# Transposes of a pair's two heads issued as one group of eight

## The chip, the cores and the metric

The kernel runs on one core of a Trainium2 chip. The metric is the device time of one execution in microseconds (us), as the median of several executions. A core has five engines that work side by side, each from a queue of its own: TensorE (PE, matrix products and transposes into the banks of PSUM), VectorE (DVE), ScalarE (ACT), GpSimd (POOL) and SyncE (SP, which here only issues DMA transfers).

## The reference

One decoder layer over 512 positions of width 1024, in float32. A first projection of the normalised input gives, among others, keys, queries, values and a gate `z` for 8 heads of 128; these go through a short causal convolution and SiLU, and then through a gated delta rule in chunks:

```python
q = l2norm(q) * DK ** -0.5;  k = l2norm(k);  beta = sigmoid(b)
g = -exp(A_log) * softplus(a + dt_bias);  G = cumsum(g)       # per chunk
L = strict_lower((k * beta) @ k.T * decay)                    # decay = exp(G_i - G_j)
u, w = solve(I + L, [v * beta, k * beta * exp(G)])
A = (q @ k.T) * decay
# scan over the chunks, state S:
v_new = u - w @ S
o     = (q * exp(G)) @ S + A @ v_new
S     = S * exp(G_last) + (k * exp(G_last - G)).T @ v_new
o = o * rsqrt(mean(o * o) + EPS) * norm_g * silu(z)
```

Beside it stand a gated convolution branch, a merge of both by sigmoid gates, and a feed-forward block with convolution; the result is normalised once more.

## The kernel before, in words

**Projections.** Weights are stored in float32. Each block of weights (1 MB, `raw`) is split on the chip into a high part `wh` (ScalarE, L139) and the rest `wl` (VectorE, L140), both of the type float32r, and a product is the sum of three (`mm3`, L115). All of them go through `mm` (L106), so the profile shows them under line 107. A job (`col_job`, L202) projects 256 columns: two groups of 24 matmuls of 512 positions, each into one bank, which is then evacuated through a convolution (`conv`, L301, steps of line 305 on VectorE).

**The order.** The author weaves the work by hand: `mm` counts the columns that it projects, and each 2048 of them (four matmuls of 512) it calls `tick` (L94). A tick advances the first generator of each of several queues by one step, `backs`, `mids`, `chains` by one and `evacs` by two; a step goes from one `yield` to the next. So the yields say how many projections stand between two steps. Some places finish a task at once instead: `reach` (L865), called in the evacuation of a key projection (L882), runs `back` of the pair two earlier to its end. The framework (Tile) then sets the waits, and orders each engine's queue at build time, in the program's order but with later instructions put ahead of those whose inputs it does not yet expect.

**The delta rule.** Heads go in four pairs. A pair has four jobs (keys, queries, values, `z`), and three generators beside them:

- `front` (L612), in `chains`: turns keys of both heads (four 128x128 transposes per head into one bank, `turn`, L606), squares them on ScalarE (L629) and writes `kn` on VectorE (L630); multiplies keys with keys and queries (L644) and scales the products to `U` and `A` (L648, L651); turns the queries and squares them (L674); waits until the values are evacuated; turns the values and writes `vs` (L682); then it inverts 16x16 blocks in `TB` on VectorE (L685 to L693) and hands them on by DMA.
- `mid` (L708), in `mids`: builds the inverse of 128x128 blocks by small products (L719 to L781), after a fixed number of ticks.
- `back` (L787), in `backs`: the scan over four chunks (L804 to L842), then a factor per position (L847, and its power on GpSimd, L848), three ticks, the scaling of the outputs (L856, four per head), their transposes (`turn`) and the product with the gate into `yb` (L861).

PSUM has eight banks of 512 floats per partition; `bank` (L79) takes one of a pool of eight, and it comes free after its last reader.

Of the kernel before, what the change touches and what calls it, by code (L numbers as in the profile page):

```python
# [59 lines left out]
def layer_kernel(ctx, tc, x, norm_mix_g, w_in, w_ab, conv_a_w, gdn_conv_w, gdn_A_log, gdn_dt_bias,  # L60
# [18 lines left out]
    def bank():  # L79
        return ps.tile([P, 512], F32, tag="ps", name=nm("ps"))  # L80
# [5 lines left out]
    def advance(queue, n):  # L86
        while n and queue:
            queue[0].step()
            if queue[0].done:
                queue.popleft()  # L90
            else:
                n -= 1
# [422 lines left out]
    def prep(pr):  # L515
        Dm = gd.tile([P, 8, P], F32, tag="Dm", name=nm("Dm"))
        nc.sync.dma_start(out=Dm, in_=gtd[8 * pr:8 * pr + 8, :].partition_broadcast(P))
        pool.affine_select(out=Dm, in_=Dm, compare_op=ALU.is_ge, fill=-1e30, base=0,
                           pattern=[[0, 8], [1, P]], channel_multiplier=-1)
        Dms[pr] = Dm  # L520

    def exps(pr):
        Dm = Dms[pr]
        for f in range(8):
            tc.keep_in_program_order(
                act.activation(out=Dm[:, f, :], in_=Dm[:, f, :], func=AF.Exp,
                               bias=negG[:, 8 * pr + f:8 * pr + f + 1]))
# [67 lines left out]
    def bc(ap, n):  # L595
        return ap.unsqueeze(2).broadcast_to([P, ap.shape[1], n])
# [6 lines left out]
    def tl(n, b=1, shape=(P, 8, P)):  # L603
        return gd.tile(list(shape), F32, tag=n, bufs=b, name=nm(n))

    def turn(src):  # L606
        o = bank()
        for n in range(NT):
            pe.transpose(out=o[:, n * P:(n + 1) * P], in_=src[:, n * P:(n + 1) * P], identity=ident)  # L609
        return o, o.rearrange("p (n d) -> p n d", d=P)  # L610

    def front(pr, st):  # L612
        kq, kqs = st["kq"], st["kqs"]
        c0 = 8 * pr
        col = lambda a, f: a[:, c0 + f:c0 + f + 1]
        if pr == 0:
            exps(0)
        Dm = Dms.pop(pr)
        ssk = tl("ssk", 2, (P, 8))
        kn = tl("kn", 2)  # L620
        junk = tl("junk", 1, (P, P))
        ap_, sk = tl("ap", 2, (P, 8)), tl("sk", 2, (P, 8))
        U, A = tl("U", 2), tl("A", 2)

        for h in range(2):
            o, ov = turn(kq[:, h, 0, :])
            yield
            for n in range(NT):
                act.activation(out=junk, in_=ov[:, n, :], func=AF.Square, accum_out=ssk[:, 4 * h + n:4 * h + n + 1])  # L629
            dve.tensor_tensor(out=kn[:, 4 * h:4 * h + 4], in0=ov,  # L630
                              in1=bc(kdv[:, c0 + 4 * h:c0 + 4 * h + 4], P), op=ALU.mult)
            yield
        dve.tensor_scalar(sk, ssk, EPS, None, op0=ALU.add)
        dve.reciprocal(out=ap_, in_=sk)
        dve.tensor_tensor(out=ap_, in0=ap_, in1=beta[:, c0:c0 + 8], op=ALU.mult)
        pool.tensor_tensor(out=sk, in0=sk, in1=phalf, op=ALU.pow)
        for h in range(2):
            for m in range(2):
                o = bank().rearrange("p (n t d) -> p n t d", n=2, t=2)
                for i in range(2):  # L640
                    n = 2 * m + i
                    sl = slice(n * P, (n + 1) * P)
                    for a, b in ((1, 0), (0, 1), (0, 0)):
                        pe.matmul(o[:, i], lhsT=kqs[:, a, h, 0, sl], rhs=kqs[:, b, h, :, sl],  # L644
                                  start=a > 0, stop=a + b == 0)
                f = h * 4 + 2 * m
                for i in range(2):
                    dve.scalar_tensor_tensor(out=U[:, f + i, :], in0=o[:, i, 0, :], scalar=ap_[:, f + i:f + i + 1],  # L648
                                             in1=Dm[:, f + i, :], op0=ALU.mult, op1=ALU.mult)
                yield  # L650
                dve.tensor_tensor(out=A[:, f:f + 2], in0=o[:, :, 1, :], in1=Dm[:, f:f + 2], op=ALU.mult)  # L651
        UB = tl("UB", 1, (64, 16, 16))
        TB = tl("TB", 1, (64, 16, 16))
        half = lambda d, e: d.rearrange("q f (e r) (g c) -> e g (q f) r c", e=2, g=2)[e, e]
        um = tl("um", 2, (P, 8, 32))
        for q in range(4):
            sl = slice(32 * q, 32 * q + 32)
            nc.sync.dma_start(out=ucd[pr][q].rearrange("f r c -> r f c"), in_=U[sl, :, sl])
        for e in range(2):
            nc.sync.dma_start(out=UB[32 * e:32 * e + 32], in_=half(ucd[pr], e))  # L660
        for q in range(4):
            sl = slice(32 * q, 32 * q + 32)
            pool.tensor_tensor(out=um[sl], in0=U[sl, :, sl],
                               in1=mask16[sl].unsqueeze(1).broadcast_to([32, 8, 32]), op=ALU.mult)
        if pr < 3:
            prep(pr + 1)
        yield

        vs, ssq = tl("vs", 2), tl("ssq", 2, (P, 8))
        for h in range(2):  # L670
            o, ov = turn(kq[:, h, 1, :])
            yield
            for n in range(NT):
                act.activation(out=junk, in_=ov[:, n, :], func=AF.Square, accum_out=ssq[:, 4 * h + n:4 * h + n + 1])  # L674
        for _ in range(Y_V):
            yield
        while "v" not in st:
            advance(evacs, 1)
        for h in range(2):
            o, ov = turn(st["vT"][:, h, :])  # L680
            yield
            dve.tensor_tensor(out=vs[:, 4 * h:4 * h + 4], in0=ov, in1=bc(sk[:, 4 * h:4 * h + 4], P), op=ALU.mult)  # L682
        yield VREAD

        dve.tensor_tensor(out=TB, in0=UB.rearrange("p j i -> p i j"), in1=nlow, op=ALU.mult)  # L685
        dve.memset(TB.rearrange("p i j -> p (i j)")[:, ::17], 1.0)
        sub = tl("sub", 1, (64, 64))
        for j in range(1, 15):
            m = 15 - j
            t = sub[:, 0:m * j].rearrange("p (i c) -> p i c", c=j)  # L690
            dve.tensor_tensor(out=t, in0=UB[:, j, j + 1:16].unsqueeze(2).broadcast_to([64, m, j]),
                              in1=TB[:, j, 0:j].unsqueeze(1).broadcast_to([64, m, j]), op=ALU.mult)
            dve.tensor_tensor(out=TB[:, j + 1:16, 0:j], in0=TB[:, j + 1:16, 0:j], in1=t, op=ALU.subtract)  # L693
            if j == Y_E and pr < 3:
                exps(pr + 1)
            if j % 3 == 0:
                yield
        for e in range(2):
            nc.sync.dma_start(out=half(tbd[pr], e), in_=TB[32 * e:32 * e + 32])
        if pr:  # L700
            mtask[pr - 1].finish()
        T = tl("T", 2, (P, 8, 32))
        for q in range(4):
            nc.sync.dma_start(out=T[32 * q:32 * q + 32], in_=tbd[pr][q].rearrange("f r c -> r f c"))
        mtask[pr] = Task(mid(pr, U, um, T, (pr, st, kn, A, ap_, vs, ssq)))
        mids.append(mtask[pr])

    def mid(pr, U, um, T, rest):  # L708
# [71 lines left out]
        for f in range(8):  # L780
            pe.matmul(o1[lo, 64 * f:64 * f + 64], lhsT=Y64[hi, f, :], rhs=TTf[hi, f, hi], start=True, stop=True)  # L781
        act.activation(out=TTf[lo, :, hi], in_=o1[lo, :].rearrange("p (f c) -> p f c", c=64),
                       func=AF.Copy, scale=-1.0)
        ctask[pr] = Task(back(*rest))
        backs.append(ctask[pr])

    def back(pr, st, kn, A, ap_, vs, ssq):  # L787
        kq = st["kq"]
# [3 lines left out]
        on = vs  # L792
        sso = tl("sso", 2, (P, 8))
        St = [None, None]
        for n in range(NT):
            sl = slice(n * P, (n + 1) * P)
            rs = []
            for h in range(2):
# [4 lines left out]
                o = bank()  # L803
# [10 lines left out]
            for h in range(2):  # L814
                f = h * 4 + n
                o = bank()
# [17 lines left out]
            for h in range(2):  # L834
                f = h * 4 + n
                o = bank()
# [16 lines left out]
        for h in range(2):  # L853
            for n in range(NT):
                f = h * 4 + n
                dve.tensor_scalar(on[:, f, :], on[:, f, :], fac[:, f:f + 1], None, op0=ALU.mult)  # L856
            yield
            yield
            o, ov = turn(on[:, 4 * h:4 * h + 4].rearrange("p n d -> p (n d)"))
            yo = yb[:, 2 * pr + h, :]  # L860
            dve.scalar_tensor_tensor(out=yo, in0=o, scalar=ng, in1=yo, op0=ALU.mult, op1=ALU.mult)  # L861

# [77 lines left out]
    st = {}  # L940
# [388 lines left out]
```

## Time and profile before

| | |
|---|---|
| time, median of 3 executions | 987.71 us (987.6 to 987.72) |
| the profiled execution | 987.75 us, span 986.0 us |
| granted TensorE clock, mean | 0.998 |
| transposes of `turn` | 128, from 45.7 to 317.6 us |

The span goes from the first to the last instruction of the profiled execution. The rows of groups and of the timeline give an instruction's line, its engine, the tiles it writes and reads (`out<-in`, without buffer numbers), its count and duration; a wait is put down to the instruction that released it. Durations of matmuls overlap, so their starts say how long each holds TensorE.

### The profile page before, as it was taken

What the parts mean: (1) busy time and instruction counts of PE and PEld (TensorE: products, weight loads), DVE (VectorE), ACT (ScalarE), POOL (GpSimd) and SP (SyncE); (2) the same over time, 40 slices, a digit from 0 to 9 for tenths busy, and PEclk for the clock granted to TensorE, in tenths of its full rate; (3) what the DMA queues carried; (4) which work ended last, traced back from release to release, by engine and by line L of the source; (5) the groups of instructions that cost most, each with busy time, mean ns of one, the idle gap of its engine ahead of it and who ended that gap; (6) DMA issues with size and microseconds to landing.
All of it is one profiled execution on the core that took longest, in us unless ns stands there. A gap on an engine that the chain in (4) does not pass through costs nothing.

```text
span 986.0 us, 15803 instructions
## 1 busy us (share of the span) xinstructions
PE 974.4 (99%) x6250; PEld 841.9 (85%) x6250; DVE 677.1 (69%) x1312; ACT 470.3 (48%) x1023; POOL 60.6 (6%) x101
## 2 busy tenths in 40 slices
PE   8999999999999999999999999999999999999997
PEld 6888887887878889999988888988999888888885
DVE  6868676796626967799753543998888888533315
ACT  7786566574344433344732332464544556322313
POOL 3320300202000000000000000000000000000000
PEclk9999999999999999999999999999999999999999
DMA  6534212222312123222533252313232224232202
GB/s 228 175 107 136 74 52 87 72 89 58 88 50 86 43 86 128 75 97 86 171 104 111 86 191 86 108 43 129 90 124 86 86 94 163 86 124 90 86 1 85
DMA packets 33466, 97.71 MB, mean 99 GB/s; under 512 B 19275, under 2 KB 19696, under 8 KB 23024
## 3 DMA queue, kind: packets, MB, share of 16 engines
q1 hardware_dynamic: 33392, 96.70, 29.5%
q8 instruction: 49, 0.80, 0.3%
q14 instruction: 25, 0.20, 0.1%
HBM read 93.27 MB, written 3.42 MB: 98 GB/s over the span
## 4 chain that ended last, share of the span: by engine, by line
PE 94%; DVE 2%; ACT 2%; issue 1%; POOL 1%; DMA 0%; SPq 0%; POOLq 0%; DVEq 0%
PE ps L107 86%; PE ps L609 1%; PE ps L644 1%; PE ps L817 1%; PE ps L837 0%; PE ps L826 0%; PE ps L781 0%; PE ps L775 0%; PE ps L805 0%; PE ps L804 0%; DMA xt<-in_x_dram 0%; PE ps L1151 0%; POOL fac L848 0%; DVE wl L140 0%; ACT hT L466 0%
## 5 line engine op out<-in xcount | busy, mean ns | idle before, releaser
L139 ACT CAST wh<-raw 128x512 fp32r<-128x512 f32 x378 | 222.4, 619 | 283.7 <-PE ps L107 243.6
L140 DVE TENSOR_TENSOR wl<-raw,wh 128x512 fp32r<-128x512 f32 x378 | 252.2, 687 | 139.5 <-ACT wh L139 137.9
L107 PE MATMUL ps<-hT,wh 128*128 128x512 f32 (+1 forms) x1104 | 318.1, 368 | 0.0
L107 PEld LDWEIGHTS ps<-hT,wh 128*128 128x128 f32 x1104 | 196.2, 189 | 27.9
L107 PE MATMUL ps<-hT,wl 128*128 128x512 f32 (+1 forms) x552 | 194.7, 362 | 0.1
L107 PE MATMUL ps<-h,wh 128*128 128x512 f32 (+1 forms) x704 | 177.9, 341 | 0.0
L107 PEld LDWEIGHTS ps<-h,wh 128*128 128x128 f32 x704 | 122.5, 189 | 15.0
L107 PEld LDWEIGHTS ps<-hT,wl 128*128 128x128 f32 x552 | 104.5, 189 | 14.2 <-DVE wl L140 0.5
L107 PE MATMUL ps<-h,wl 128*128 128x512 f32 (+1 forms) x352 | 114.6, 341 | 0.0
L107 PE MATMUL ps<-wh,as 128*128 128x512 f32 x352 | 108.4, 389 | 0.0
L107 PEld LDWEIGHTS ps<-wh,as 128*128 128x128 f32 x352 | 66.1, 188 | 13.7
L107 PEld LDWEIGHTS ps<-h,wl 128*128 128x128 f32 x352 | 66.7, 190 | 7.6
L107 PE MATMUL ps<-wl,as 128*128 128x512 f32 x176 | 68.5, 389 | 0.0
L107 PE MATMUL ps<-ts,wh 128*128 128x256 f32 x320 | 59.2, 283 | 0.0
L305 DVE SCALAR_TENSOR_TENSOR cv<-ps,wA,cv 128x511 f32<-128x511 f32 (+2 forms) x72 | 53.2, 740 | 3.2 <-ACT cv L302 2.9
L107 PEld LDWEIGHTS ps<-ts,wh 128*128 128x128 f32 x320 | 50.6, 192 | 0.0
L160 DVE TENSOR_TENSOR raw<-raw 128x512 f32<-128x512 f32 x72 | 49.4, 687 | 0.9
L107 PE MATMUL ps<-us,wh 128*128 128x256 f32 x256 | 47.4, 283 | 0.0
L107 PEld LDWEIGHTS ps<-us,wh 128*128 128x128 f32 x256 | 40.5, 192 | 0.0
L107 PE MATMUL ps<-ts,wl 128*128 128x256 f32 x160 | 40.1, 283 | 0.0
L107 PE MATMUL ps<-wh,mix 128*128 128x512 f32 x128 | 40.1, 391 | 0.0
L107 PE MATMUL ps<-yas,wh 128*128 128x512 f32 x128 | 39.6, 389 | 0.0
(260 smaller groups left out, 1302.1 us busy)
## 6 DMA issues: line engine op xcount, KB each, us to landing
raw<-in_w_in_dram SPq DMA_DIRECT2D x36, 1024.0 KB, 5.0
raw<-in_w_up_dram SPq DMA_DIRECT2D x22, 1024.0 KB, 4.9
raw<-in_w_down_dram SPq DMA_DIRECT2D x11, 1024.0 KB, 4.9
raw<-in_w_a_out_dram SPq DMA_DIRECT2D x4, 1024.0 KB, 4.9
raw<-in_w_b_out_dram SPq DMA_DIRECT2D x4, 1024.0 KB, 4.9
raw<-in_w_o_dram SPq DMA_DIRECT2D x4, 1024.0 KB, 4.9
Dm<-gtd SPq DMA_DIRECT2D x4, 512.0 KB, 4.2
x<-in_x_dram SPq DMA_DIRECT2D x4, 512.0 KB, 6.7
```

The lines of the kernel that those rows point to most:

```text
L107: pe.matmul(o, lhsT=a, rhs=b, start=start, stop=stop, skip_group_check=free)
L139: act.copy(out=wh, in_=src)
L140: dve.tensor_tensor(out=wl, in0=src, in1=wh.bitcast(F32), op=ALU.subtract)
L160: dve.tensor_tensor(out=r[q], in0=a, in1=b, op=op)
L305: dve.scalar_tensor_tensor(out=dst[:, sh:], in0=src[:, :S - sh], scalar=wcol(j), in1=dst[:, sh:], op0=ALU.mult, op1=ALU.add)
L609: pe.transpose(out=o[:, n * P:(n + 1) * P], in_=src[:, n * P:(n + 1) * P], identity=ident)
L644: pe.matmul(o[:, i], lhsT=kqs[:, a, h, 0, sl], rhs=kqs[:, b, h, :, sl], start=a > 0, stop=a + b == 0)
L817: pe.matmul(o[:, 0:P], lhsT=TTf[:, f, :], rhs=rs[h], start=True, stop=True)
```

## The change

In four places `turn` is now called for both heads in a row, ahead of the loop over the heads, so that eight transposes stand together in the program, in two banks; before, a head's four transposes were followed by a `yield` (or two, for the outputs) and its evacuation, and then came the other head. The loops over the heads keep the evacuation. The yields around them change: keys have one behind the group and one per head, queries one behind the group and one per head, values one behind the group, outputs one per head behind its scaling and two ahead of the group. No computation is changed.

```diff
-        for h in range(2):
-            o, ov = turn(kq[:, h, 0, :])
-            yield
+        turned = [turn(kq[:, h, 0, :])[1] for h in range(2)]
+        yield
+        for h, ov in enumerate(turned):
             for n in range(NT):
                 act.activation(out=junk, in_=ov[:, n, :], func=AF.Square, accum_out=ssk[:, 4 * h + n:4 * h + n + 1])
             dve.tensor_tensor(out=kn[:, 4 * h:4 * h + 4], in0=ov,
...
-        for h in range(2):
-            o, ov = turn(kq[:, h, 1, :])
-            yield
+        turned = [turn(kq[:, h, 1, :])[1] for h in range(2)]
+        yield
+        for h, ov in enumerate(turned):
             for n in range(NT):
                 act.activation(out=junk, in_=ov[:, n, :], func=AF.Square, accum_out=ssq[:, 4 * h + n:4 * h + n + 1])
+            yield
         for _ in range(Y_V):
             yield
         while "v" not in st:
             advance(evacs, 1)
-        for h in range(2):
-            o, ov = turn(st["vT"][:, h, :])
-            yield
+        turned = [turn(st["vT"][:, h, :])[1] for h in range(2)]
+        yield
+        for h, ov in enumerate(turned):
             dve.tensor_tensor(out=vs[:, 4 * h:4 * h + 4], in0=ov, in1=bc(sk[:, 4 * h:4 * h + 4], P), op=ALU.mult)
         yield VREAD
...
                 dve.tensor_scalar(on[:, f, :], on[:, f, :], fac[:, f:f + 1], None, op0=ALU.mult)
             yield
-            yield
-            o, ov = turn(on[:, 4 * h:4 * h + 4].rearrange("p n d -> p (n d)"))
+        yield
+        yield
+        turned = [turn(on[:, 4 * h:4 * h + 4].rearrange("p n d -> p (n d)"))[0] for h in range(2)]
+        for h, o in enumerate(turned):
             yo = yb[:, 2 * pr + h, :]
             dve.scalar_tensor_tensor(out=yo, in0=o, scalar=ng, in1=yo, op0=ALU.mult, op1=ALU.mult)
```

## The prediction

> **What bounds the kernel now.** I read the page first, then TensorE's waits, then the timeline around the transposes.
>
> ```profile
> span 986.0 us, 15803 instructions
> PE 974.4 (99%) x6250; PEld 841.9 (85%) x6250; DVE 677.1 (69%) x1312; ACT 470.3 (48%) x1023; POOL 60.6 (6%) x101
> PE 94%; DVE 2%; ACT 2%; issue 1%; POOL 1%; DMA 0%; SPq 0%; POOLq 0%; DVEq 0%
> ```
>
> TensorE is busy for 99% of the span and holds 94% of the chain that ends last. So an edit counts only by what it does to TensorE's queue: instructions fewer or shorter, or waits that go or come. Next, what TensorE waited for (us in total, times, longest), and the transposes of `turn` by what they turn:
>
> ```profile
> PE ps L609 <- DVE vs L856: 2.0, 3, 0.8
> PE ps L728 <- DVE U L648: 0.5, 1, 0.5
> L609 PE MATMUL ps<-ident,kq x64: 270/272/329, 45.7 to 232.5; 128*128 128x128 f32 x64
> L609 PE MATMUL ps<-ident,vT x32: 270/272/330, 63.2 to 242.7; 128*128 128x128 f32 x32
> L609 PE MATMUL ps<-ident,vs x32: 270/272/331, 140.2 to 317.6; 128*128 128x128 f32 x32
> ```
>
> 128 transposes stand in 32 groups of four. Behind the start-up the only waits of TensorE of half a microsecond or more in total are these two, and the larger belongs to the lines that the change moves: the transposes of the outputs wait for VectorE's scaling (L856).
>
> **What a switch between projections and transposes costs.** The timeline of TensorE around the outputs of pair 2, where nothing waits (start, duration):
>
> ```profile
> 266.65 0.39 PE L107 MATMUL ps<-hT,wh 128*128 128x512 f32 x1
> 266.88 0.39 PE L107 MATMUL ps<-hT,wl 128*128 128x512 f32 x1
> 267.11 0.60 PE L609 MATMUL ps<-ident,vs 128*128 128x128 f32 x4
> 267.46 0.48 PE L107 MATMUL ps<-hT,wh 128*128 128x512 f32 x1
> 267.77 0.39 PE L107 MATMUL ps<-hT,wl 128*128 128x512 f32 x1
> 268.00 0.40 PE L107 MATMUL ps<-hT,wh 128*128 128x512 f32 x1
> 268.24 0.40 PE L107 MATMUL ps<-hT,wl 128*128 128x512 f32 x1
> ```
>
> Read starts, not durations: matmuls overlap. A projection of 512 columns takes 0.23 (266.65 to 266.88). From 266.88 to 268.00 are 1.12 us with three projections in it, 0.69, so the four transposes cost 0.43. Inside a group they start (0.60 - 0.27) / 3 = 0.11 apart, and four of that are 0.44. The late first projection behind the group (267.46 to 267.77 is 0.31, not 0.23) is paid back by its early start (0.35 after the group's, not 0.44). So the switch itself costs nothing that I can read, and one or two steps of 0.24 behind it up to 0.03. A group of eight for two of four saves that once: 16 merges (four pairs, four kinds) by 0 to 0.03 are 0 to 0.5 us. I take **0.2**.
>
> **What moves.** The work beside the projections runs in ticks: one per 2048 projected columns, four steps of 0.23, 0.92 us. Count the yields of `front` around its turns. Keys: four before, three after (one behind the group, one per head). Queries: two before, three after, since a yield is added per head. Values: two before, one after. So the products and the queries come a tick earlier, the values' first group at the tick of before, and what follows the values (TB, then `mid`, then `back`) one tick earlier against the projections, in each pair. `back` keeps four yields between its first scaling and its last transposes. No DMA is added; the loads and stores of U, TB and T are issued in the same order, U's a tick earlier behind the keys, TB's and T's behind the values. SP's queue and POOL's (pow, masks) pass nothing they did not pass before. The same 128 transposes, 64 squares and 24 evacuations stay.
>
> **The term that decides: the outputs of pairs 0 and 1.** These two `back` tasks are not ticked to their end: the key projection two pairs later finishes them (`reach(pr - 2, 99)`, L882), so their yields do not space them there. Pair 0, then pair 1:
>
> ```profile
> 137.82 0.17 DVE L847 SCALAR_TENSOR_TENSOR fac<-sso,ssq 128x8 f32<-128x8 f32 x1
> 138.07 1.64 POOL L848 TENSOR_TENSOR fac<-fac,nhalf 128x8 f32<-128x8 f32 x1 [21.89 <-DVE fac L847]
> 139.24 0.39 PE L107 MATMUL ps<-hT,wl 128*128 128x512 f32 x1
> 139.74 0.88 DVE L856 TENSOR_SCALAR vs<-vs,fac 128x128 f32<-128x128 f32 x4 [1.76 <-POOL fac L848]
> 140.17 0.83 PE L609 MATMUL ps<-ident,vs 128*128 128x128 f32 x4 [0.55 <-DVE vs L856]
> 140.53 0.75 DVE L305 SCALAR_TENSOR_TENSOR cv<-ps,wA,cv 128x511 f32<-128x511 f32 x1
> 141.19 0.28 DVE L856 TENSOR_SCALAR vs<-vs,fac 128x128 f32<-128x128 f32 x1
> 141.62 0.30 PE L609 MATMUL ps<-ident,vs 128*128 128x128 f32 x1 [0.61 <-DVE vs L856]
> 143.36 0.67 DVE L856 TENSOR_SCALAR vs<-vs,fac 128x128 f32<-128x128 f32 x3
> 144.42 0.38 PE L609 MATMUL ps<-ident,vs 128*128 128x128 f32 x2
> ```
>
> ```profile
> 195.88 1.64 POOL L848 TENSOR_TENSOR fac<-fac,nhalf 128x8 f32<-128x8 f32 x1 [9.04 <-DVE fac L847]
> 196.68 0.40 PE L107 MATMUL ps<-hT,wh 128*128 128x512 f32 x1
> 197.55 1.46 DVE L856 TENSOR_SCALAR vs<-vs,fac 128x128 f32<-128x128 f32 x7 [1.16 <-POOL fac L848]
> 197.89 0.33 PE L609 MATMUL ps<-ident,vs 128*128 128x128 f32 x1 [0.81 <-DVE vs L856]
> ```
>
> POOL's power takes 1.64 us and VectorE's scaling waits for it. TensorE has come to the transposes by 139.24 + 0.23 = 139.47 and starts at 140.17: 0.70 lost. The four would let the fifth start at 140.17 + 0.44 = 140.61; it starts at 141.62: 1.01 lost. Pair 1: 196.68 + 0.23 = 196.91 against 197.89: 0.98. Together **2.69 us**, which is all that can be won here. (TensorE's order, a single transpose and then projections and then two more, shows that the framework orders the queue at build time by when it expects inputs; real time is late against that.) Pairs 2 and 3 are ticked normally and do not wait:
>
> ```profile
> 263.90 1.66 DVE L856 TENSOR_SCALAR vs<-vs,fac 128x128 f32<-128x128 f32 x8 [1.82 <-POOL fac L848]
> ```
>
> With the change `back` of pair 0 is a tick (0.92) further when it is finished by force. Its power ends at 139.71 - 0.92 = 138.79. The eight scalings, in a row as in pair 2, take 1.66, from 138.8 to 140.5, and the first four are ready when TensorE arrives at 139.47. It could start the last of eight at 139.47 + 7 x 0.11 = 140.24; its input is there at about 140.5. So 0.3 is lost where 1.71 were: 1.4 won; with the convolution step of 0.75 still between the heads 0.7 won. Pair 1: scalings from 197.55 - 0.92 = 196.63 to 198.29, last transpose due at 196.91 + 0.77 = 197.68: 0.6 lost where 0.98 were, 0.4 won, or up to 0.9 if projections are put between. Sum 1.1 to 2.3; I take **1.9**, near the upper half, because the first wait of each pair goes in every order that I can construct.
>
> **Costs that I put at nothing.** Keys: the four squares of one head and their reads keep ScalarE
>
> ```profile
> L629 ACT ACTIVATE junk<-ps 128x128 f32<-128x128 f32 x32 | 9.0, 281 | 2.6 <-PE ps L609 2.1
> L629 ACT ACTIVATION_READ_ACCUMULATOR junk<-ps 128x1 f32 x32 | 6.5, 203 | 0.0
> ```
>
> for 4 x (0.28 + 0.20) = 1.9 us, two ticks, but the heads now come one tick apart. The products of keys and queries (L644) then start before their scale is known, and their banks are held a tick longer: 0 to 0.9 us per pair if a bank is missing, below nothing excluded since nothing is taken away. I take 0, because TensorE shows no wait for a bank now; both ends are in the rivals.
>
> Sum: 0.2 + 1.9 = 2.1 us off the profiled execution of 987.75 us (span 986.0), which lies 0.04 above the median of 987.71. **Forecast 985.6 us**; its own range from 984.9 (2.69 + 0.2 off) to 986.6 (1.1 off).
>
> **Rivals.** *The wait only changes its place* (20%). Eight transposes need eight scalings, 1.66 us, where four needed 0.88; if the queue is ordered so that all eight stand together ahead of the projections, or the earlier tick does not reach POOL (VectorE's queue holds L847 back in pair 1, where convolution and values stand ahead of it), pair 0 loses about 1.2 and pair 1 1.5: 2.7 as now, so 987.5. For it: the forced finish. Against it: the power's input is a tick earlier in the program.
>
> *Slower: banks run out* (18%). Place: pair 0, where the exponentials come late.
>
> ```profile
> 49.37 0.87 PE L644 MATMUL ps<-kqs 128*128 128x256 f32 x6
> 56.83 0.60 PE L609 MATMUL ps<-ident,kq 128*128 128x128 f32 x4
> 58.02 0.64 DVE L648 SCALAR_TENSOR_TENSOR U<-ps,ap,Dm 128x128 f32<-128x128 f32 x2 [1.00 <-ACT Dm L526]
> 58.20 0.60 PE L609 MATMUL ps<-ident,kq 128*128 128x128 f32 x4
> 58.58 0.41 DVE L651 TENSOR_TENSOR A<-ps,Dm 128x256 f32<-128x256 f32 x1
> 61.12 0.41 DVE L651 TENSOR_TENSOR A<-ps,Dm 128x256 f32<-128x256 f32 x1
> ```
>
> Four banks with L644's products are held from 49.4 on, the first until 58.99, the last until 61.5; the queries take two more, one is being projected into and one evacuated: eight of eight at the worst moment. The second head's bank is now wanted at 56.83 + 0.44 = 57.3, not at 58.2. If none is free, TensorE stands until 58.99: 1.7 us; in the other pairs, where the products come one tick before their scale, up to 0.9 each: 1.7 + 2.7 = 4.4, so 985.6 + 4.4 = 990.0. It decides as soon as banks cost more than the 2.1 won. The Trainium skill (Perfetto Trace Analysis, Identifying Performance Opportunities) says that the same gap repeating on the engine that should be saturated can mean that there is no room in SBUF or PSUM for the next tile; by that rule a group that asks for two banks at once would show such a gap at each of its 16 places. The trace of before agrees only in that it has none: 0 waits of a transpose for a bank.
>
> *Slower: the moved tick makes other steps collide* (12%). `mid` and `back` move against the projections' convolutions on VectorE; the nearest row is the 0.5 us wait of L728 for L648. Some four to eight of these, 2 to 4 us, eat the gain: 987.6 to 989.6.
>
> **How the numbers follow.** Forecast 50%, of which 40 lie below 985.73, 0.2% under the median (about what a measurement of this kernel tells from no change), and 10 above. Wait in another place 20%, same. Banks 18%: 15 slower, 3 same. Collisions 12%: 2 faster by luck, 3 same, 7 slower; that gives 42, 36 and 22. The range must leave out no more than 2 in 10: from 984.8, just under the forecast's own end, to 990.0.
>
> **What would show it.** Right: the total that L609 waits for L856 falls from 2.0 below 1.0, in pairs 0 and 1 the first wait is gone; groups of eight take 0.87 us start to start; L817 of each pair starts about 0.9 us earlier against the projections. Wrong: waits of L609 or L107 for ACT or DVE readers of ps (L629, L651, L674), or new waits at L728, L826, L817; or L856 waits at L609 as long as before.

## The result, and the profile after

The changed kernel takes **985.64 us** (median of 12 executions, 985.23 to 985.86) where the kernel before took 987.72 beside it: a ratio of 0.9978, 95% interval 0.9969 to 0.9987. The profiled execution's span fell from 986.0 to 984.0 us. The first rows of the page of the changed kernel:

```profile
span 984.0 us, 15795 instructions
PE 974.1 (99%) x6250; PEld 842.3 (86%) x6250; DVE 678.8 (69%) x1312; ACT 470.0 (48%) x1023; POOL 60.2 (6%) x101
```

The number of instructions on each engine and TensorE's busy time (974.4 before) are what they were. Of the 2.0 us by which the span is shorter, 1.7 are idle time of TensorE (986.0 - 974.4 = 11.6 before, 984.0 - 974.1 = 9.9 now), and TensorE's waits say which (columns: us in total, times, longest; lines behind 674 have moved, L856 is now L857, L728 is L729):

```profile
PE ps L430 <- DVE warm L394: 1.5, 1, 1.5
PE ps L609 <- DVE vs L857: 0.5, 1, 0.5
PE ps L473 <- DMA wr<-in_norm_mix_g_dram: 0.4, 1, 0.4
PE ps L456 <- DVE xr L451: 0.4, 1, 0.4
```

Of the outputs' wait one piece of 0.5 is left of 2.0 in three pieces, and the wait of L728 for 0.5 us is not there any more. The timeline of pair 0, all engines, shows how (start, duration, and in brackets the idle time ahead):

```profile
137.60 1.64 POOL L849 TENSOR_TENSOR fac<-fac,nhalf 128x8 f32<-128x8 f32 x1 [22.19 <-DVE fac L848]
...
139.28 1.46 DVE L857 TENSOR_SCALAR vs<-vs,fac 128x128 f32<-128x128 f32 x7 [1.75 <-POOL fac L849]
...
139.69 0.39 PE L107 MATMUL ps<-hT,wl 128*128 128x512 f32 x1
139.91 1.21 PE L609 MATMUL ps<-ident,vs 128*128 128x128 f32 x7
140.66 0.74 DVE L305 SCALAR_TENSOR_TENSOR cv<-ps,wA,cv 128x511 f32<-128x511 f32 x1
141.32 0.27 DVE L857 TENSOR_SCALAR vs<-vs,fac 128x128 f32<-128x128 f32 x1
...
141.65 0.33 PE L609 MATMUL ps<-ident,vs 128*128 128x128 f32 x1 [0.53 <-DVE vs L857]
```

TensorE is due at 139.69 + 0.23 = 139.92 and starts at 139.91: the first wait is gone. The power starts 139.91 - 137.60 = 2.31 us ahead of that moment, where it was 139.47 - 138.07 = 1.40 before: 0.91 more, one tick. But only seven scalings stand together; a convolution step (L305) went ahead of the eighth, and TensorE, which has the eighth transpose next, starts it at 141.65. Seven transposes from 139.91 would let it start at 139.91 + 0.77 = 140.68: 0.97 lost, where 1.71 were. Pair 1:

```profile
193.55 1.64 POOL L849 TENSOR_TENSOR fac<-fac,nhalf 128x8 f32<-128x8 f32 x1 [7.91 <-DVE fac L848]
...
195.90 1.65 DVE L857 TENSOR_SCALAR vs<-vs,fac 128x128 f32<-128x128 f32 x8
...
196.25 0.39 PE L107 MATMUL ps<-hT,wh 128*128 128x512 f32 x1
196.48 0.27 PE L609 MATMUL ps<-ident,vs 128*128 128x128 f32 x1
...
196.82 0.49 PE L609 MATMUL ps<-ident,vs 128*128 128x128 f32 x3
```

Here the scaling does not even wait for the power (no bracket), and TensorE loses nothing where it lost 0.98. Note that the "group of eight" is not one in this place: the framework laid projections between the transposes, one, three, three and one.

### The profile page after: what moved, and what is told of

It reads as the page before. It is cut to its first block, busy times and chain, and to the rows that moved or that the text cites. A ratio compares the mean times of both kernels' runs of the same rounds, so it can differ in the third digit from the quotient of the medians.

```text
span 984.0 us, 15795 instructions
## 1 busy us (share of the span) xinstructions
PE 974.1 (99%) x6250; PEld 842.3 (86%) x6250; DVE 678.8 (69%) x1312; ACT 470.0 (48%) x1023; POOL 60.2 (6%) x101
## 4 chain that ended last, share of the span: by engine, by line
PE 94%; ACT 3%; DVE 1%; issue 1%; DMA 0%; POOL 0%; SPq 0%; POOLq 0%
PE ps L107 86%; PE ps L609 1%; PE ps L644 1%; PE ps L818 1%; PE ps L838 1%; PE ps L827 0%; ACT Dm L526 0%; PE ps L806 0%; PE ps L805 0%; PE ps L782 0%; PE ps L776 0%; DMA xt<-in_x_dram 0%; PE ps L1154 0%; ACT wh L139 0%; PE ps L720 0%
## 5 line engine op out<-in xcount | busy, mean ns | idle before, releaser
L305 DVE SCALAR_TENSOR_TENSOR cv<-ps,wA,cv 128x511 f32<-128x511 f32 (+2 forms) x72 | 53.2, 740 | 4.7 <-ACT cv L302 4.5
```

The costliest lines, as they stand in the source:

```text
L305: dve.scalar_tensor_tensor(out=dst[:, sh:], in0=src[:, :S - sh], scalar=wcol(j), in1=dst[:, sh:], op0=ALU.mult, op1=ALU.add)
```

## The experiments

Three theories were tried. **Theory 1**: the gain is the tick, that is, the forced outputs of pairs 0 and 1 find their scaling done because `back` runs one tick earlier. **Theory 2**: it is the grouping, fewer switches of TensorE between projections and transposes. **Theory 3**: it is the outputs' own order, both heads' scalings ahead of both heads' transposes. Each run is compared with the kernel before on the same chip. Three constants set the ticks in some of them: `Y_V` ticks stand ahead of the values in `front`, `Y_T` ahead of `mid`, and `Y_M` further ones ahead of `mid` of pair 0.

### The ticks without the groups

```diff
                               in1=bc(kdv[:, c0 + 4 * h:c0 + 4 * h + 4], P), op=ALU.mult)
-            yield
+            if h == 1:
+                yield
         dve.tensor_scalar(sk, ssk, EPS, None, op0=ALU.add)
...
                 act.activation(out=junk, in_=ov[:, n, :], func=AF.Square, accum_out=ssq[:, 4 * h + n:4 * h + n + 1])
+            if h == 0:
+                yield
...
             o, ov = turn(st["vT"][:, h, :])
-            yield
+            if h == 0:
+                yield
```

Expected:

> The kernel before, every transpose in its old groups of four with projections between, but with the yields of front set so that the products come a tick earlier, the values at their old tick, and TB, mid and back a tick earlier, as in the changed kernel. Theory 1 (the tick, now in front and mid together, so that the blocks T are also sent a tick earlier): 985.4 to 986.0, as the changed kernel. Theory 2 (fewer switches): 987.5 or more.

Measured: 985.8 us, ratio 0.9979 (0.9971 to 0.9988), the gain of the changed kernel. TensorE's waits in it:

```profile
PE ps L609 <- DVE vs L860: 0.5, 1, 0.5
```

The program issues every transpose in its old group of four (two pairs of groups came to stand next to each other in TensorE's queue, so its trace has 33 stretches of transposes, where the kernel before has 35 and the changed kernel 20). The wait has shrunk from 2.0 to 0.5 all the same, and that of L728 is gone. Theory 1 is borne out, and theory 2 falls as the main cause.

### The groups without the ticks

Keys, queries and values are grouped as in the changed kernel, the outputs are as before, and yields put every later step back to its tick; the lines are shown against the changed kernel:

```diff
                               in1=bc(kdv[:, c0 + 4 * h:c0 + 4 * h + 4], P), op=ALU.mult)
             yield
+        yield
         dve.tensor_scalar(sk, ssk, EPS, None, op0=ALU.add)
...
                 act.activation(out=junk, in_=ov[:, n, :], func=AF.Square, accum_out=ssq[:, 4 * h + n:4 * h + n + 1])
-            yield
+            if h == 0:
+                yield
...
             dve.tensor_tensor(out=vs[:, 4 * h:4 * h + 4], in0=ov, in1=bc(sk[:, 4 * h:4 * h + 4], P), op=ALU.mult)
+        yield
         yield VREAD
```

Expected:

> The kernel before with keys, queries and values in groups of eight, but with yields added so that the products, the values, TB, mid and back keep the tick that they had. Theory 1: no gain, 987.5 to 987.9, with the waits of L609 for the scaling as before (2.0 us). Theory 2: three quarters of the gain, 986.1. Theory 3: no gain, 987.7.

Measured: 989.25 us, ratio 1.0022 (1.0013 to 1.0031): no gain, and slower than any theory said. Its waits:

```profile
PE ps L609 <- DVE vs L860: 2.1, 3, 1.0
...
PE ps L732 <- DVE TT L716: 1.1, 1, 1.1
...
PE ps L732 <- issue: 0.3, 1, 0.3
```

The outputs wait as before, which is theory 1's part. The 1.1 us are at the line that was L728, in pair 2, where 0.5 stood before; the profile puts them down to VectorE's transpose of T (L712 before). T itself is sent later here, as SyncE's rows show (221.98 in the kernel before):

```profile
217.52 0.35 SPq L134 DMA_DIRECT2D raw<-in_w_in_dram  x1
218.56 0.86 SPq L703 DMA_DIRECT2D tbd<-TB  x2
223.55 1.78 SPq L708 DMA_DIRECT2D T<-tbd  x4
```

The stores of TB (`tbd<-TB`), which T is read from, left 1.0 us behind the load of a weight block (L134) and landed 4.5 us after their issue; in the kernel before they landed after 2.1. The run after the next comes back to this.

### Only the tick of `mid` and `back`

```diff
-Y_V, Y_T, Y_G, Y_N, Y_E, SLAB = 4, 17, 16, 3, 4, 4
+Y_V, Y_T, Y_G, Y_N, Y_E, SLAB = 4, 16, 16, 3, 4, 4
```

Expected:

> The kernel before, with mid started one tick earlier (Y_T 17 to 16) and every transpose in its old groups of four. Theory 1 (the gain is the tick: back runs 0.9 us earlier, so the power on GpSimd is ready when the outputs of pairs 0 and 1 are forced out): about 985.8 us, and the waits of L609 for L856 fall from 2.0 us to under 0.8. Theory 2 (the gain is in fewer switches between projections and transposes): no change, 987.7. Theory 3 (the gain is that both heads' scalings stand ahead of both heads' transposes): no change, 987.7.

Measured: 990.01 us (single executions from 987.57, at a mean granted clock of 0.999, to 992.89, at 0.995), ratio 1.0023 (1.0012 to 1.0034). Its waits:

```profile
PE ps L728 <- issue: 3.0, 1, 3.0
PE ps L430 <- DVE warm L394: 1.5, 1, 1.5
PE ps L728 <- DVE TT L712: 1.1, 1, 1.1
PE ps L719 <- DMA T<-tbd: 1.0, 1, 1.0
PE ps L609 <- DVE vs L856: 0.3, 1, 0.3
```

The outputs did what theory 1 says: 0.3 instead of 2.0. Up to 215 us of the span this kernel had gained 1.9 us on the one before, projection for projection (the same projection starts at 215.42 before and at 213.23 here, of which 0.24 is the start-up). At 320 us, behind the last transposes, it was 4.1 us late, so it had lost 6.3 in pair 2: waits of 3.0, 1.1 and 1.0 us, and a stretch at half the clock that the last section shows. `mid` came a tick earlier, but T hardly did: it was sent at 221.23 instead of 221.98, although the projections were 2.19 us ahead. L719 waits for the DMA of the blocks T, and L728 for their transpose. So the time of theory 1 failed though its mechanism held, and a second condition showed up: T must come earlier too.

### One tick earlier from the values on

```diff
-Y_V, Y_T, Y_G, Y_N, Y_E, SLAB = 4, 17, 16, 3, 4, 4
+Y_V, Y_T, Y_G, Y_N, Y_E, SLAB = 3, 17, 16, 3, 4, 4
```

Expected:

> The kernel before with one tick less ahead of the values (Y_V 4 to 3): values, TB, mid and back come a tick earlier, but the products of keys and queries keep their tick; groups of four. Theory 1: the outputs' waits shrink by 1.7 us as in the changed kernel. If the wait of L728 in pair 2 went because the products came a tick earlier, it is not gone here but about 0.9 us longer, and the time is 986.5 to 987.5; if it went with the tick of mid alone, 985.7.

Measured: 991.25 us (single executions from 987.79 to 992.17), ratio 1.003 (1.0019 to 1.0042), far above what was expected. Its waits, without the start-up:

```profile
PE ps L728 <- issue: 1.9, 1, 1.9
...
PE ps L728 <- DVE TT L712: 1.3, 1, 1.3
PE ps L719 <- DMA T<-tbd: 0.8, 1, 0.8
...
PE ps L609 <- DVE vs L856: 0.7, 2, 0.5
```

The outputs' wait shrank by 1.3, and that of L728 grew about as expected, from 0.47 us (put down to L648) to 1.34 (to the transpose), but T's DMA came late as well, which I had thought the earlier TB would prevent. So what keeps pair 2 whole is the other half of the change's yields, the one that the keys lose ahead of the products. SyncE's rows of pair 2 show how: first the kernel before (with the first use of T), then this run, then the changed kernel.

```profile
215.92 0.35 SPq L134 DMA_DIRECT2D raw<-in_w_in_dram  x1
219.36 0.86 SPq L699 DMA_DIRECT2D tbd<-TB  x2
221.98 1.78 SPq L704 DMA_DIRECT2D T<-tbd  x4
...
224.84 0.24 PE L719 MATMUL ps<-T,um 32*32 32x32 f32 x2
```

```profile
216.19 0.35 SPq L134 DMA_DIRECT2D raw<-in_w_in_dram  x1
217.24 0.86 SPq L699 DMA_DIRECT2D tbd<-TB  x2
222.22 1.78 SPq L704 DMA_DIRECT2D T<-tbd  x4
```

```profile
214.11 0.83 SPq L700 DMA_DIRECT2D tbd<-TB  x2
215.06 0.42 SPq L134 DMA_DIRECT2D raw<-in_w_in_dram  x1
216.49 1.78 SPq L705 DMA_DIRECT2D T<-tbd  x4
```

TB did come earlier in this run: its stores left 2.1 us before those of the kernel before (217.24 against 219.36). But they landed 4.5 us after their issue instead of 2.1, so T was sent no earlier. What stands ahead of them is the load of a weight block of 1 MB (L134), 1.0 us here and 3.4 in the kernel before, and T is sent 6.0 and 6.1 us behind that load. It is so in all six kernels whose products keep their tick: the load stands ahead of TB's stores, these land 1.8 to 4.7 us after their issue, T is sent 5.8 to 6.3 us behind the load, and L719 or L728 waits. In the six whose products come a tick earlier, TB's stores stand ahead of the load and land after 1.9 to 2.0 us, and neither line waits.

So one yield fewer ahead of the products matters because the long chain of small steps on VectorE (L685 to L693) finds another place: it ends five microseconds earlier, not one, and its stores pass ahead of the weights. With that the earlier `mid` does no harm. Two things are not shown: why the framework then lays the chain elsewhere, and, by a run of its own, that the load is what delays the stores; no run moves the load alone.

### The changed kernel, a tick later

```diff
-Y_V, Y_T, Y_G, Y_N, Y_E, SLAB = 4, 17, 16, 3, 4, 4
+Y_V, Y_T, Y_G, Y_N, Y_E, SLAB = 4, 18, 16, 3, 4, 4
```

Expected:

> The changed kernel, all groups of eight kept, with mid started one tick later (Y_T 17 to 18), so that back stands against the projections as in the kernel before. Theory 1: the first wait of pairs 0 and 1 is back, 987.3 us or more. Theory 2: 985.6, as the changed kernel. Theory 3: 985.6 to 986.

Measured: 987.25 us, ratio 0.9996 (0.9988 to 1.0005). All groups of eight are kept, and the outputs' wait is back where it was:

```profile
PE ps L609 <- DVE vs L857: 2.0, 3, 0.9
```

The wait of L728 stayed away, which would be the half microsecond by which the median is lower; the interval does not exclude that nothing is left of the gain.

### The changed kernel with the outputs as before

```diff
-            yield
-        yield
-        yield
-        turned = [turn(on[:, 4 * h:4 * h + 4].rearrange("p n d -> p (n d)"))[0] for h in range(2)]
-        for h, o in enumerate(turned):
+            yield
+            yield
+            o, ov = turn(on[:, 4 * h:4 * h + 4].rearrange("p n d -> p (n d)"))
```

Expected:

> The changed kernel with the outputs as before (two groups of four, each behind its own scaling), keys, queries and values in groups of eight, the tick kept. Theory 1: most of the gain stays, 985.6 to 986.2. Theory 2: a quarter of the gain is lost, 986.2. Theory 3: the gain is gone, 987.3 or more.

Measured: 985.8 us, ratio 0.9981 (0.9972 to 0.999). The gain stays: theory 3 falls.

### The outputs alone grouped

The same edit the other way round, in the kernel before. Expected:

> The kernel before with the outputs alone as in the changed kernel: eight scalings, then eight transposes; keys, queries, values and all ticks as before. Theory 1: the first waits of pairs 0 and 1 stay as they are (0.7 and 1.0 us), 987.3 to 988.0. Theory 3 (the gain is that both heads' scalings stand ahead of both heads' transposes): 986.0 or less.

Measured: 987.71 us, ratio 0.9999 (0.999 to 1.0008). No gain, and the waits of the kernel before stand in it unchanged:

```profile
PE ps L609 <- DVE vs L856: 2.0, 3, 0.8
...
PE ps L728 <- DVE U L648: 0.5, 1, 0.5
```

### The power taken out of the chain

```diff
-        pool.tensor_tensor(out=fac, in0=fac, in1=nhalf, op=ALU.pow)
+        dve.tensor_scalar(fac, fac, 1.0, None, op0=ALU.mult)
```

Expected:

> The kernel before with the power on GpSimd (1.64 us, line 848) left out of the outputs' factor: a copy on VectorE stands in its place, so the outputs lack the power of -1/2. No tick and no group is changed. Theory 1: the factor is ready 1.6 us earlier and the waits of the outputs' transposes go, 985.1 to 985.8 (up to 2.7 us won). Theories 2 and 3: no change, 987.5 to 987.9.

Measured: 985.85 us, ratio 0.9983 (0.9974 to 0.9992), single executions from 985.11 to 987.9. The waits, without the start-up, of the execution that was profiled, one of 987.34 us:

```profile
PE ps L728 <- DVE TT L712: 1.0, 1, 1.0
...
PE ps L719 <- DMA T<-tbd: 0.3, 1, 0.3
PE ps L728 <- issue: 0.2, 1, 0.2
```

No transpose of an output waits at all: GpSimd's 1.64 us were the cause of the outputs' wait. But part of what was won is given back in pair 2: TensorE, less delayed, comes to L719 and L728 before T, which goes by VectorE and DMA. In the profiled execution the granted clock then fell to 0.50 for 3.4 us, as the last section shows. The four executions above 986.5 us had a mean granted clock of 0.996 or 0.997, the seven others 0.998 or 0.999.

### Pair 0 a further tick earlier

```diff
-Y_M = 10
+Y_M = 9
```

Expected:

> The changed kernel with mid and back of pair 0 alone one tick earlier (Y_M 10 to 9); its blocks T land 2 us before they are used. Theory 1: what is left of the wait in pair 0 (0.97 us) goes too, 984.7 to 985.0. Theory 2: no change, 985.6.

Measured, with the changed kernel as base: **984.33 us**, ratio 0.9964 (0.9952 to 0.9977) to the kernel before. TensorE waits for nothing behind the start-up, and the eight transposes of pair 0 run in one piece (timelines of TensorE and VectorE):

```profile
139.53 1.03 PE L609 MATMUL ps<-ident,vs 128*128 128x128 f32 x8
```

```profile
138.00 1.66 DVE L857 TENSOR_SCALAR vs<-vs,fac 128x128 f32<-128x128 f32 x8 [1.76 <-POOL fac L849]
```

It is 1.3 us under the changed kernel, 0.4 to 0.7 lower than expected. The wait of pair 0 accounts for 0.97 of it; where the rest came from I did not trace.

### The same without the groups

The run of the ticks without the groups, with Y_M at 9. Expected:

> The ticks of the changed kernel with groups of four (as the ticks-without-groups run), and pair 0 a further tick earlier (Y_M 9). If groups of eight are worth nothing: 984.2 to 984.6, as the changed kernel with Y_M 9. If they are worth the 0.2 to 0.5 us of fewer switches: 984.6 to 985.0.

Measured: 984.65 us, ratio 0.9969 (0.9957 to 0.9981). That is just inside the second range, but the intervals of this run and the one with groups overlap. With groups the medians are 0.16 (985.64 against 985.8) and 0.32 us (984.33 against 984.65) lower, but the kernels of each pair were not measured side by side: against the kernel before that ran beside each, the gains are 2.08 with groups and 2.10 without, and 3.57 and 2.98 with Y_M at 9. The starts of one and the same projection in the traces tell more. From 20 us on, which leaves out the start-up, to the projection that starts at 320.06 us in the kernel before, TensorE gained 2.09 us with groups and 1.97 without, and 3.55 and 3.32 with Y_M at 9. So the grouping is worth 0.12 and 0.23 us in these four executions, one of each kernel, and the measured times do not tell it clear of zero.

## Why the prediction was right

The number was right (985.6 forecast, 985.64 measured), and so was the step that it hung on, the tick. That the two numbers agree within 0.04 us is luck: the parts of the sum were off by more, as the points on the outputs and on the costs show. Term by term:

- **What bounds it.** Right: TensorE's count and busy time did not move, its waits did.
- **Switches between projections and transposes: 0.2 forecast.** The traces with and without groups give 0.12 and 0.23, the times give nothing clear of zero. Right, as far as it can be told.
- **The tick.** Right: the power of pair 0 starts 0.91 us earlier against the projections, one tick. In pair 1 it is 196.48 - 193.55 = 2.93 us ahead instead of 196.91 - 195.88 = 1.03, two ticks' worth; in VectorE's queue the factor (L847) now stands behind one convolution step after the scan, where it stood behind two and a write of the values. The scan itself came as forecast: in every pair its first matmul (L817) stands four projections earlier on TensorE, one tick (behind 440 instead of 444 matmuls of line 107 in pair 0, 592 instead of 596, 784 instead of 788, and 928 instead of 932 in pairs 1 to 3).
- **The outputs: 1.9 forecast, 1.72 measured,** but the shares were the other way round. Pair 0 gave 1.71 - 0.97 = 0.74, not 1.4: the convolution step stands in the row, ahead of the eighth scaling, which is the lower of the two cases that I had named. Pair 1 gave 0.98, not 0.4: projections were laid between the transposes, the upper case.
- **Costs put at nothing.** Here something was missed, on both sides. The products' earlier tick, which I costed at nothing or a loss, removed the wait of L728 (0.5 us), and it is what makes the rest of the change possible: without it the same tick of `mid` costs 2.3 us (`mid` and `back` alone) or 3.6 (from the values on). I had named this wait as the place where moved ticks might collide, but did not see that T's DMA of pair 2 stood right at its limit before, sent at 221.98 and used from 224.84 on. And the prediction had SyncE's queue pass nothing that it did not pass before; in fact TB's stores pass ahead of a weight load there, five microseconds earlier. The sum came out right because 0.5 us that I had not counted (L728) and some 0.3 of small losses, of which I traced only 0.16 at the values of pair 0, nearly balanced the 0.2 that the outputs gave less than forecast.
- **The rivals.** The wait that only changes its place: wrong, the first wait of both pairs is gone. Banks: the changed kernel has no wait of TensorE that the profile puts down to a reader of a bank. The Trainium skill (Perfetto Trace Analysis, Identifying Performance Opportunities) says that the same gap repeating on the engine that should be saturated can mean a lack of room in PSUM; the trace of the changed kernel agrees in that it has no such gap: behind the start-up the only wait listed is the 0.5 us of pair 0. Collisions after the moved tick: wrong for this change, but right for two experiments that moved the same tick in another way, which were 2.3 and 3.6 us slower.

## What to carry to other kernels

Where steps are woven into a saturated engine's queue by hand, a change of grouping also changes when everything behind it comes: count the yields before the switches, and test the order and the delay by separate kernels. A slow operation on a side engine (here one power of 8 columns, 1.64 us) cost something only where a step was forced out early, and moving the yields alone won what the whole regrouping won. Moving only some of them lost 2.3 and 3.6 us. So before moving a consumer forward, look at the transfer that feeds it last: if it lands just in time, its producer has to move too, and it matters what stands ahead of the producer's stores in the DMA queue.

## What the runs showed of the hardware that I had not expected

In the run with `mid` and `back` alone a tick earlier, TensorE stood still in the middle of the matmuls of L728, for 3.04 us that the profile puts down to nothing, after 1.1 and 1.0 us for TT and T. Projections behind it then ran at about half speed for a while, as the timeline shows:

```profile
230.72 0.26 PE L728 MATMUL ps<-Y,TT 32*32 32x32 f32 x2 [3.04 <-issue]
...
232.78 0.63 PE L107 MATMUL ps<-hT,wl 128*128 128x512 f32 x1
...
233.21 0.63 PE L107 MATMUL ps<-hT,wh 128*128 128x512 f32 x1
```

They start 0.43 apart instead of 0.23. The rows by window give the length of a stretch, TensorE's busy time in it, and the granted clock (PEclk, the third number from the right); first this run, then the one with the power left out:

```profile
224.65:228.06 3.41, 1.93 (x127) 1.60 (x126) 2.94 (x9) 0.89 (x2) 0.00 (x0) 1.00 0.84 286
228.06:234.89 6.83, 4.17 (x38) 3.26 (x39) 1.81 (x5) 0.81 (x2) 2.52 (x6) 0.50 0.12 26
```

```profile
224.61:228.02 3.41, 2.16 (x127) 1.84 (x116) 3.38 (x11) 0.78 (x2) 1.28 (x2) 1.00 0.75 259
228.02:231.43 3.41, 3.41 (x17) 2.27 (x17) 0.31 (x1) 2.51 (x11) 3.09 (x7) 0.50 0.43 99
```

The granted clock was 0.50 for 6.8 and 3.4 us, where it is 1.00 in the kernel before. TensorE had 4.2 and 3.4 us of work in these stretches, so half the clock cost about 2.1 and 1.7 us, an estimate from these rows. The Trainium skill (TensorE: Matmul & The Clock Gate, Part 1) says that the array falls to half its clock after about 3.4 us of idleness. The trace agrees with the half, but not with one idle stretch of that length: in the first run the clock fell 0.4 us into the hole (227.68 to 230.72), and in the second no wait was longer than 1.0 us. In the 3.4 us ahead of the fall TensorE was busy for 1.9 and 2.2 us, in the first run for 1.45 of them with 32x32 matmuls of L719 and L728. So waits of one microsecond around such small matmuls can cost more than themselves. These runs give no threshold: where the groups stood without the ticks, 2.0 us of work in 3.4 (227.1 to 230.5) left the clock at 1.00.

What the 3.04 us were is open; similar holes of 1.9, 0.3 and 0.2 us stand at the same place in the runs that were a tick earlier from the values on, with the groups but not the ticks, and without the power.
